# Layer 1's merge gates as seven block products in pairs, and four smaller edits, in a two-layer hybrid attention kernel

## The chip, the cores and the metric

The kernel runs on one core of one Trainium2 chip, as one program. The metric is its device time in microseconds; less is better. Of the core's engines the text speaks of PE (TensorE matmul; PEld is its weight load), DVE (VectorE), ACT (ScalarE), POOL (GpSimd), and SP, whose queue issues the DMA transfers.

## The reference, cut to what matters

Two layers are computed over 512 latent tokens (width 1024); 256 context tokens are also updated in layer 0, and only read in layer 1.

```python
h = rms_norm(x, norm_g) * (1 + scale) + shift
qc, kvc, kr, dq, dk, dv, sq, sk, sv, z, gm = split_cols(h @ w_in)      # one input projection
ya = dense_attend(...)      # mla: qc (384) and kvc (256) are RMS-normed first, then projected up
yb = diff_post(diff_attend(...))
yc = swa_latent(...)
def merge_branches(ys, z, gm, w_branch, w_out):
    for r, y in enumerate(ys):                       # 3 branches, z and gm have 3*1024 columns
        terms.append(sigmoid(gm_r) * ((y * silu(z_r)) @ w_branch[r]))
    return (terms[0] + terms[1] + terms[2]) @ w_out
x = x + gate * merge_branches(...)
return rms_norm(x, final_norm)                       # after layer 1
```

## The kernel before, in words

Everything is float32. For a matmul each operand is split into a rounded part H and a rest L, and a product is three matmuls (`PASS`: H·H, H·L, L·H). ACT writes H, DVE writes L as "source minus H" (`split_to`, and `split` in `weight_stream` for weights). A weight block of 128 output columns is a tile `ws` as loaded, and two tiles `wh` (H and L) after the split; six `wh` tiles go round. The activations h lie in 16 tiles `s` (8 of 128 features, H and L), with the context tokens in columns 0 to 255 and the latents in 256 to 767.

**The order of the work.** A planner (`Plan`) runs while the program is built: generators yield the time from which they can go on, `P.tick` and `P.advance` move its clock by a cost for each matmul (`mm_cost`), and every engine's instructions are emitted in the order in which it takes them. On the chip each engine runs its instructions strictly in that order, and waits on semaphores. PE's order interleaves two streams: the attention units (`stream_a`) and the projections (`stream_b`). Stream b's order is written out by hand: `SEQ[l]` for the first part of layer l (Q, K, V: the windowed branch; c0 to c2, cn, p: mla's queries; l0, l1, ln, u, w: mla's keys and values; k, q, v: the differential branch; z20 and so on: silu gates computed early), then `MID` in layer 0 and `BR` in layer 1 for the merge. Short PE work that hangs on a chain goes through `P.pe` as a piece, which is taken before the streams as soon as it is ready. `HAM` and `advance` model that matmuls cost double after a stretch in which PE did little.

**The merge in layer 0** (`gates_by_pairs`). z (silu gate) and g (merge gate) of two blocks of 128 columns are computed together: the two weight blocks are cut in halves of the features, h in halves of the features and of the tokens, and instead of eight block products seven are made (a Winograd form). `seven` makes four sums of weight halves (S1 to S4) and splits all seven operands, 11 DVE operations on 128x512 for each pair; `sums` makes the sums of h (T1 to T4) once. `pair_entry` issues seven products of 12 matmuls over half the tokens (384 columns each), and its `chain` puts the results together with one ACT copy and seven DVE additions, while PE goes on. The results go to DRAM (`s_d`, `g_d`), and come back when `u_entry` (y·silu(z)) and `b_entry` (times `w_branch`, times the gate) need them.

**The merge in layer 1** (`gates`). Eleven of the 24 z blocks are in `SEQ[1]`. The other 13, and all 24 g blocks, are computed one at a time by `wide`: 24 matmuls of 512 columns each, into one of two wide banks (`wd`).

**The other places that the change touches.** `rms_cols` normalises the latents of mla: it sums squares over partitions with matmuls of two columns against `ones` (each stands as two in the trace), then takes the root and spreads it by transposes. `s_pieces` scores one row of 128 queries at a time; a differential row takes both wide banks, one for each of its two maps. `begin` loads the first rows and the modulation weights. `out_entry` ends with the final norm.

Of the kernel before, what the change touches and what calls it, by code (L numbers as in the profile page):

```python
# [16 lines left out]
F32 = mybir.dt.float32  # L17
# [10 lines left out]
INF = float("inf")  # L28
NS, NT, NWS, NWH = 46, 9, 2, 6
MID = 'z25 z26 z27 z16 t z17 z00 z01 T pg20g21+ pg22g23+ pg24g25+ pg26g27+ pz02z03+ pz04z05+ pz06z07+ pg10g11+ pg12g13+ u20 pg14g15+ u21 pg16g17+ u22 pg00g01+ u23 pg02g03+ u24 pg04g05 u25 pg06g07! u26 u27 b20 b21 u10 u11 b22 u12 u13 b23 u14 b24 u15 b25 u16 b26 u17 b27 u00 u01 b10 u02 u03 b11 u04 u05 b12 u06 b13 u07 b14 b15 b16 b17 b00 b01 b02 b03 b04 b05 b06 b07'  # L30
BR = ['z0 z3 g0 z7 z4 z5 z2 z6 g2 z1 g5 b0 b2 g1 g4 g3 b3 b1 b4 g6 g7 b6 b5 b7', 'z7 z0 z5 z2 g0 g2 z4 z1 z3 g1 z6 g4 b1 g3 b0 b4 g5 g6 b3 b5 b6 g7 b2 b7', 'z4 z0 z7 z1 z2 z6 g0 z3 z5 g2 g1 g3 g6 g4 g5 b1 b3 b2 b4 g7 b0 b5 b6 b7']
# [9 lines left out]
DEPTH = 2  # L41
START = 1
# [3 lines left out]
SEQ = ["cn Q0 K0 V Q1 c0 c2 c1 Q2 Q3 cr p1 z20 p2 p0 p3 Q4 z21 K1 Q5 z22 Q6 z23 k1 Q7 v0 k0 v1 q0 z24 q1 k3 q2 k2 l0 v2 l1 ln lr q3 q5 k4 q4 k5 v3 k6 q6 u0 q7 k7 w0 z11 z10 u1 w1 z12 w2 z13 z14 u2 z15 u3 w3",  # L46
       "K0 V cn Q0 Q1 c1 c0 c2 Q2 cr p0 p1 Q3 p2 p3 z20 Q4 K1 z21 Q5 z22 Q6 z23 Q7 v0 l0 k0 q0 k1 z24 v1 k2 q1 q2 q3 l1 lr k3 q4 v2 ln k4 k5 q5 v3 k6 q6 k7 q7 u0 z10 w0 z11 u1 z12 z13 u2 w2 w1 z15 z14 u3 w3"]
# [81 lines left out]
class Plan:  # L129
# [43 lines left out]
    def pe(self, ready, cost, emit):  # L173

        done = When()
        self.pieces.append((ready, cost, emit, done))
        yield done
        return done.t

    def advance(self, cost):  # L180
# [15 lines left out]
    def run(self, a, b):  # L196
# [8 lines left out]
        while live or self.pieces or self.waiting:  # L205
            self.flush()
            for i, (ready, cost, emit, done) in enumerate(self.pieces):
                if at(ready) <= self.now - TOPE:
                    del self.pieces[i]
                    emit()  # L210
                    self.advance(cost)
# [25 lines left out]
def hybrid_kernel(tc, x_in, c_in, ctx_in, c_ctx, w_mod, b_mod, norm_g, w_in, q_norm, w_uq, kv_norm, w_ukv,  # L237
# [645 lines left out]

    def normalise(t, p, r):
# [23 lines left out]
    def soft_diff(u, row, m, p, rel, t):  # L908
        lo, hi = u["span"]
# [46 lines left out]
    def s_pieces(u):  # L956
        for row in u["rows"]:
            row["t"] = When()
# [5 lines left out]
            maps = 2 if u["kind"] == "diff" else 1  # L964
            yield lambda: max(wd.gate(maps), at(u["ready"]), at(row["ready"]), room(2)())
# [355 lines left out]
    def rms_cols(raw, sq, nt, nfeat, gcol, outH, outL, done, times, tk0=0):  # L1321
# [4 lines left out]
        def emit():  # L1326
            o["p"], o["r"] = bk.take()
            for i in range(ntk):
                for k in range(nt):
                    c = (i + tk0) * 128  # L1330
                    mm(o["p"][:, 2 * i:2 * i + 2], sq[k][:, c:c + 128], ones, k == 0, k == nt - 1)
        t = yield from P.pe(lambda: max([bk.gate()] + [w.t for w in times]), nt * ntk * 215.0, emit)
# [40 lines left out]
    def build_layer(o):  # L1373
# [851 lines left out]
```

## Time and profile before

| | us |
|---|---|
| three runs | 2669.98, 2665.61, 2669.41 (median 2669.41) |
| the profiled execution | 2665.98, span 2664.2 |
| PE busy | 2594.5 (97% of the span), 16419 matmuls |
| DVE busy | 1750.0 (66%) |
| ACT busy | 1386.0 (52%) |
| mean granted TensorE clock | 0.994 |

PE is busy in 97% of the span, so the time is PE's work plus the places at which PE stands still or runs at a lower clock. The span falls into the start (0 to 45 us), layer 0's attention with projections (45 to 1010), its merge (1010 to 1490), the step to layer 1 (1490 to 1540), layer 1's attention with projections (1540 to 2292), its merge (2292 to 2655) and the tail.

### The profile page before, as it was taken

The numbers are of one execution on the slowest core, as the hardware profiler recorded it, in microseconds if no ns is written. First come the engines' busy times: TensorE is split into PE (matmuls) and PEld (weight loads), VectorE is DVE, ScalarE is ACT, GpSimd is POOL, SyncE is SP. The second block draws the span as 40 slices with busy tenths as digits, with TensorE's granted clock in tenths as the row PEclk, the third lists the DMA queues.
The fourth block names the chain that finished last, engine by engine and source line by source line (L and its number), as shares of the span: only waits on it lengthen the run. The fifth ranks groups of instructions, "written<-read, shape, count | busy, mean of one in ns | idle before, by whom it ended". The sixth has DMA issues, their size and how long they took to land. (4 is left out here: it accounts for less than half of the span.)

```text
span 2664.2 us, 42925 instructions
## 1 busy us (share of the span) xinstructions
PE 2594.5 (97%) x16419; PEld 2284.4 (86%) x16419; DVE 1750.0 (66%) x3292; ACT 1386.0 (52%) x2791; POOL 172.1 (6%) x371
## 2 busy tenths in 40 slices
PE   7999999999999999999999999999999999999998
PEld 5988898888889888899888888898888789888887
DVE  4777786757786657677454478887577777534535
ACT  5667775646665543344222267776555656422323
POOL 1110110111110000000000011110110100000000
PEclk9999999999999999999999999999999999999999
DMA  7223211121122545455753423222211233344433
GB/s 243 49 77 108 67 45 52 45 59 29 52 82 73 170 150 154 145 159 162 245 204 111 134 78 103 78 57 61 60 50 44 62 94 105 106 125 126 127 97 132
DMA packets 341009, 274.48 MB, mean 103 GB/s; under 512 B 26134, under 2 KB 297588, under 8 KB 340804
## 3 DMA queue, kind: packets, MB, share of 16 engines
q1 hardware_dynamic: 340160, 271.41, 34.4%
q8 instruction: 129, 2.11, 0.3%
q14 instruction: 76, 0.62, 0.1%
q0 software_dynamic: 416, 0.30, 0.1%
q10 hardware_dynamic: 228, 0.03, 0.0%
HBM read 221.72 MB, written 49.95 MB: 102 GB/s over the span
## 5 line engine op out<-in xcount | busy, mean ns | idle before, releaser
L530 PE MATMUL bk<-s,wh 128*128 128x512 f32 (+2 forms) x5262 | 1052.4, 350 | 19.5 <-DVE pt L324 14.4
L530 PEld LDWEIGHTS bk<-s,wh 128*128 128x128 f32 x5262 | 852.3, 189 | 122.6 <-DVE pt L324 21.8
L324 DVE TENSOR_TENSOR wh<-ws,wh 128x1024 fp32r<-128x1024 f32 (+4 forms) x305 | 312.9, 1031 | 352.2 <-ACT wh L310 350.6
L530 PE MATMUL wd<-s,wh 128*128 128x512 f32 (+1 forms) x2616 | 537.2, 367 | 2.9 <-ACT s L310 2.7
L530 PEld LDWEIGHTS wd<-s,wh 128*128 128x128 f32 x2616 | 452.2, 189 | 84.2 <-ACT s L310 3.3
L310 ACT ACTIVATE wh<-ws 128x1024 fp32r<-128x1024 f32 (+4 forms) x305 | 273.0, 900 | 390.4 <-PE wd L530 252.7
L310 ACT ACTIVATE pt<-bk 128x512 fp32r<-128x512 f32 (+4 forms) x619 | 348.5, 580 | 170.6 <-PE bk L1000 113.4
L324 DVE TENSOR_TENSOR pt<-bk,pt 128x512 fp32r<-128x512 f32 (+4 forms) x469 | 295.7, 645 | 83.4 <-ACT pt L310 66.4
L530 PE MATMUL bk<-wh,s 128*128 128x256 f32 (+1 forms) x2304 | 331.3, 295 | 1.0 <-DVE pt L324 0.4
L530 PEld LDWEIGHTS bk<-wh,s 128*128 128x128 f32 x2304 | 300.1, 191 | 11.7 <-DVE pt L324 1.1
L530 PE MATMUL bk<-pt,s 128*128 128x256 f32 x1888 | 279.3, 287 | 8.4 <-DVE pt L324 6.4
L530 PEld LDWEIGHTS bk<-pt,s 128*128 128x128 f32 x1888 | 252.9, 191 | 31.3 <-DVE pt L324 14.7
L530 PE MATMUL wd<-s,s 128*128 128x256 f32 (+5 forms) x1872 | 270.5, 329 | 1.8 <-ACT s L310 1.6
L310 ACT ACTIVATE s<-wd,ti 128x768 f32<-128x768 f32 (+1 forms) x240 | 195.3, 817 | 126.6 <-DVE ti L912 73.8
L530 PEld LDWEIGHTS wd<-s,s 64*128 64x128 f32 (+2 forms) x1872 | 210.8, 188 | 29.2 <-issue 6.2
L1000 PE MATMUL bk<-ident,s 128*128 128x128 f32 x1472 | 209.1, 274 | 4.9 <-DVE s L324 1.7
L310 ACT ACTIVATE s<-s,ti 128x513 f32<-128x513 f32 (+6 forms) x256 | 184.0, 726 | 27.1 <-DVE ti L948 13.2
L1000 PEld LDWEIGHTS bk<-ident,s 128*128 128x128 f32 x1472 | 170.7, 142 | 26.0 <-DVE s L331 3.3
L310 ACT ACTIVATE s<-s 128x768 fp32r<-128x768 f32 (+2 forms) x98 | 75.2, 768 | 198.3 <-DVE s L324 178.4
L310 ACT ACTIVATE yo<-bk 128x256 f32<-128x256 f32 (+1 forms) x200 | 72.4, 383 | 158.6 <-PE bk L530 157.6
L310 ACT ACTIVATE s<-bk 128x256 fp32r<-128x256 f32 (+6 forms) x305 | 119.7, 426 | 61.1 <-PE bk L530 59.7
L948 DVE CUSTOM_DVE_ANT_0 s<-wd,s,sinkt 128x512 f32<-128x512 f32 (+2 forms) x160 | 116.2, 745 | 48.4 <-PE wd L530 48.1
(115 smaller groups left out, 1828.6 us busy)
## 6 DMA issues: line engine op xcount, KB each, us to landing
ws<-in_w_in_dram SPq DMA_DIRECT2D x167, 512.0 KB
ws<-in_w_branch_dram SPq DMA_DIRECT2D x48, 512.0 KB
s<-s SPq DMA_DIRECT2D x48, 384.0 KB
s<-in_w_mod_dram SPq DMA_DIRECT2D x48, 256.0 KB
s<-in_w_mod_dram SPq DMA_DIRECT2D x32, 384.0 KB
y<-yo SPq DMA_DIRECT2D x80, 128.0 KB
g<-s SPq DMA_DIRECT2D x24, 384.0 KB
s<-y SPq DMA_DIRECT2D x24, 384.0 KB
```

Source lines behind the costliest of these rows:

```text
L310: lambda: nc.scalar.activation(out=out, in_=in_, func=func, scale=scale, **kw))
L324: t = yield from dve(ready, lambda: nc.vector.tensor_tensor(out=out, in0=a, in1=b, op=op), n)
L530: nc.tensor.matmul(o, lhsT=l, rhs=r, start=first, stop=last)
L948: t = yield from dve(t, lambda: nc.vector.tensor_tensor_reduce(out=pt_[:, 0:n], in0=p[:, lo:hi], in1=mk, scale=1.0, scalar=sk, op0=ALU.add ...
L1000: nc.tensor.transpose(out=pp[:, j * 256 + ri2 * 128:j * 256 + ri2 * 128 + 128], in_=row["P"][:, c:c + 128], identity=ident)
```

## The change

1. **Layer 1's gates as pairs.** `gates` and `BR` are gone; the code of `gates_by_pairs` now serves both layers, with halves of 256 tokens in layer 1. `MID[1]` sets the order: the 13 remaining z first, each by the ordinary `z_pre` (512 columns, result to DRAM), with the sums T1 to T4 (`t`) and six u among them, then 12 pairs of g, then u and b. T2 and T3 of layer 1 are written over the context columns of h.
2. **First loads.** `keep_busy` gives PE eight groups of four transposes of the identity, planned from 29 us on, 1.1 us apart. They use a bank and wait for nothing else.
3. **Context rows.** The eight differential units over context queries score both rows of queries at once (`score_two`): both rows of a map lie in one wide bank.
4. **Latent norms.** In `rms_cols` the sums over partitions are issued in groups of two token blocks, as pieces of their own, and the planner counts a tenth of their time as PE activity.
5. **Order.** Both `SEQ` lists are other orders of the same steps. In the final norm the multiplication by `final_norm` stands behind the sum for the root instead of ahead of it.

```diff
-MID = 'z25 z26 z27 z16 t z17 ...'
-BR = ['z0 z3 g0 z7 z4 z5 z2 ...']
+MID = ['z25 z26 z27 z16 t z17 ...', 'z25 z26 z27 t z16 z17 z00 u20 z01 u21 z02 u22 z03 u23 z04 u24 z05 u25 z06 z07 pg20g21+ pg22g23+ pg24g25+ pg26g27+ pg10g11+ pg12g13+ pg14g15+ pg16g17+ pg00g01+ pg02g03+ pg04g05+ u26 u27 pg06g07+! u10 u11 b20 u12 b21 u13 b22 ...']
...
+WARM = (29000.0, 1100.0, 8)
...
-SEQ = ["cn Q0 K0 V Q1 c0 c2 c1 Q2 Q3 cr p1 z20 ...", "K0 V cn Q0 Q1 c1 c0 c2 Q2 cr p0 ..."]
+SEQ = ['Q0 K0 V Q1 c2 c0 c1 Q2 cn Q3 p1 z20 cr ...', 'K0 V Q0 Q1 c0 c1 c2 Q2 cn cr p1 ...']
...
-            self.ham[i] = self.ham.get(i, 0.0) + d / f
+            self.ham[i] = self.ham.get(i, 0.0) + d / f * share
...
+    def score_two(rows):
+        o = [wd.take() for _ in range(2)]
+        ps_ = [[row["passes"](m) for m in range(2)] for row in rows]
+        for j in range(2):
+            for i in range(len(ps_[0][0])):
+                for m in range(2):
+                    q, k = ps_[j][m][i]
+                    mm(o[m][0][:, 512 * j:512 * j + 256], q, k[:, 0:256], i == 0, i == len(ps_[0][0]) - 1)
...
-        def emit():
-            o["p"], o["r"] = bk.take()
-            for i in range(ntk):
...
-        t = yield from P.pe(lambda: max([bk.gate()] + [w.t for w in times]), nt * ntk * 215.0, emit)
+        for i0 in range(0, ntk, 2):
+            def emit():
+                if i0 == 0:
+                    o["p"], o["r"] = bk.take()
+                for i in range(i0, min(i0 + 2, ntk)):
...
+            t = yield from P.pe(lambda: max([bk.gate() if i0 == 0 else 0.0] + [w.t for w in times]), nt * min(2, ntk - i0) * 112.0, emit, 0.1)
...
+                    else:
+                        XB["T2"][s][k], XB["T3"][s][k] = hs[i][k][:, 0:hw], hs[i][k + 4][:, 0:hw]
...
-        (gates_by_pairs if cx else gates)()
...
-                        if l == 1:
+                        if l == 1 and not final:
                             t = yield from tt(t, x, x, o.fn[h][0][:, cc:cc + n], ALU.mult)
...
                             t, r = yield from rstd(t2, s4[tk][:, 0:c + 1])
+                            t = max(t, (yield from tt(t2, x, x, o.fn[h][0][:, cc:cc + n], ALU.mult)))
...
+    def keep_busy():
+        for i in range(WARM[2]):
+            def emit():
+                p, r = bk.take()
+                for c in range(4):
+                    nc.tensor.transpose(out=p[:, c * 128:c * 128 + 128], in_=ident, identity=ident)
+                r.t = P.now
+            yield from P.pe(lambda: max(WARM[0] + i * WARM[1], bk.gate()), 448.0, emit)
```

How the change moves instructions, at the places that the prediction speaks of.

**PE, at the end of layer 1's attention.** Names: `bk` and `wd` are banks, `pt` and `s` data, `wh` split weights. Before, the last product of attention (128x256, into `bk`) is followed by the wide blocks, 1401 matmuls of 512 columns:

```order
L530 MATMUL bk_68<-pt_25160,s_24478 128x256
L530 MATMUL bk_68<-pt_25155,s_24479 128x256
L530 MATMUL wd_71<-s_16278,wh_24632 128x512
L530 MATMUL wd_71<-s_16279,wh_24632 128x512
L530 MATMUL wd_71<-s_16278,wh_24633 128x512
L530 MATMUL wd_71<-s_16280,wh_24632 128x512
```

Now, behind attention, 249 of these (z) stand into `bk`, then the pairs, 1008 matmuls of 256 columns in one stretch, then 576 of 512 columns (b). The step from z to the pairs:

```order
L529 MATMUL bk_66<-s_16314,wh_25567 128x512
L529 MATMUL bk_66<-s_16315,wh_25567 128x512
L529 MATMUL bk_66<-s_16314,wh_25568 128x512
L529 MATMUL bk_69<-s_16300,wh_25617 128x256
L529 MATMUL bk_69<-s_16301,wh_25617 128x256
L529 MATMUL bk_69<-s_16300,wh_25618 128x256
```

Over the whole program the 24 g blocks (576 matmuls of 512 columns) are replaced by the 1008 of 256, and the 13 z move from `wd` to `bk`.

**DVE, in the same part.** Before, for each block of 512 columns one split of a weight (`wh`, 128x1024) and one to three operations on a result:

```order
L324 TENSOR_TENSOR wh_26639<-ws_26567,wh_26638 128x1024
L324 TENSOR_TENSOR wh_26674<-ws_26603,wh_26673 128x1024
L331 SCALAR_TENSOR_TENSOR s_26633<-s_26633,wd_71 128x512
L324 TENSOR_TENSOR s_26633<-s_26633,s_26631 128x512
L331 SCALAR_TENSOR_TENSOR s_26634<-s_26633,s_26631 128x512
L324 TENSOR_TENSOR wh_26710<-ws_26642,wh_26709 128x1024
```

Now 18 operations for each pair: 11 on weights of the next pair (128x512) and seven that read a bank and add (128x256). From one pair:

```order
L323 TENSOR_TENSOR s_26133<-ws_26131,s_26133 128x512
L323 TENSOR_TENSOR pt_26233<-bk_67,pt_26231 128x256
L323 TENSOR_TENSOR wh_26314<-ws_26131,wh_26313 128x512
L323 TENSOR_TENSOR ws_26131<-pt_26281,ws_26131 128x512
L323 TENSOR_TENSOR pt_26232<-bk_66,pt_26231 128x256
L323 TENSOR_TENSOR pt_26282<-ws_26131 128x512
L323 TENSOR_TENSOR s_26229<-bk_67,pt_26232 128x256
```

The third addition of a pair (`pt_26232<-bk_66`, after the fourth product) now stands behind the split of the next pair's A11 and the sum S2; it frees the bank that the seventh product takes.

**PE, the norm of mla's queries in layer 0.** The rows `<-ones` are the sums over partitions. Before, 18 of them stand in one stretch; its last three and what follows:

```order
L530 MATMUL bk_67<-ones,s_1070 128x2
L530 MATMUL bk_67<-ones,s_1400 128x2
L530 MATMUL bk_67<-ones,s_1072 128x2
L530 MATMUL bk_66<-pt_1577,s_687 128x256
L530 MATMUL bk_66<-pt_1582,s_687 128x256
```

Now they stand in three groups of six, with four attention products of 256 columns between two groups; from the end of the first group:

```order
L529 MATMUL bk_68<-ones,s_1104 128x2
L529 MATMUL bk_68<-ones,s_1430 128x2
L529 MATMUL bk_68<-ones,s_1102 128x2
L529 MATMUL bk_69<-pt_1607,s_719 128x256
L529 MATMUL bk_69<-pt_1612,s_719 128x256
```

In layer 1 the norm of the keys' latents stays one stretch of 12 such rows, as before; in layer 0 it is now three groups of four.

**PE, the first loads.** Before, the last modulation weights (`sil`), the columns (`selt`) and the first projection:

```order
L666 MATMUL bk_69<-s_305,sil 32x512
L666 MATMUL bk_69<-s_307,sil 32x512
L678 MATMUL bk_67<-selt,pt_435 128x2 x4
L530 MATMUL bk_68<-s_160,wh_437 128x512
L530 MATMUL bk_68<-s_161,wh_437 128x512
```

Now, with the transposes (`<-ident`) in between; three more groups of four stand ahead of this piece, and two behind it:

```order
L665 MATMUL bk_69<-s_305,sil 32x512
L2135 MATMUL bk_68<-ident 128x128 x4
L665 MATMUL bk_69<-s_307,sil 32x512
L2135 MATMUL bk_66<-ident 128x128 x4
L677 MATMUL bk_67<-selt,pt_454 128x2 x4
L2135 MATMUL bk_68<-ident 128x128 x4
L529 MATMUL bk_66<-s_160,wh_446 128x512
```

More of the change, by code (lines that the diff above doesn't have):

```diff
@@ L171, in on, with pe, advance @@
         return t + 135.0
[L173 removed]
+    def pe(self, ready, cost, emit, share=1.0):
         done = When()
[L176 removed]
+        self.pieces.append((ready, cost, emit, done, share))
         yield done
         return done.t
[L180 removed]
+    def advance(self, cost, share=1.0):
         while cost > 0.0:
@@ L206, in run @@
             self.flush()
-            for i, (ready, cost, emit, done) in enumerate(self.pieces):
+            for i, (ready, cost, emit, done, share) in enumerate(self.pieces):
                 if at(ready) <= self.now - TOPE:
@@ L210, in run @@
                     emit()
-                    self.advance(cost)
+                    self.advance(cost, share)
                     done.t = self.now + 200.0
@@ L908, in soft_diff @@
     def soft_diff(u, row, m, p, rel, t):
-        lo, hi = u["span"]
+        lo, hi = row.get("span", u["span"])
         n = hi - lo
@@ L957, in s_pieces @@
         for row in u["rows"]:
+            if "span" in row:
+                continue
             row["t"] = When()
@@ L964, in s_pieces, with both @@
             maps = 2 if u["kind"] == "diff" else 1
+            if u["kind"] == "diff" and len(u["kts"]) == 2:
+                if row is not u["rows"][0]:
+                    continue
+                u["rows"][1].update(t=When(), Pm=[None, None], tm=[When(), When()], i=1)
+                yield lambda: max(wd.gate(2), at(u["ready"]), room(4)())
+                for j, r_ in enumerate(u["rows"]):
+                    r_["span"] = (512 * j, 512 * j + 256)
+                for m, (p, rel, t) in enumerate(score_two(u["rows"])):
+                    half = [When(), When()]
+                    def both(half=half, rel=rel):
+                        yield lambda: max(w.t for w in half)
+                        rel.t = max(w.t for w in half)
+                    for r_, h_ in zip(u["rows"], half):
+                        P.spawn(soft_diff(u, r_, m, p, h_, t), RANK[1])
+                    P.spawn(both(), 0)
+                continue
             yield lambda: max(wd.gate(maps), at(u["ready"]), at(row["ready"]), room(2)())
@@ L1793, in all_ @@
[L1793 to L1805 removed]
+                    else:
+                        XB["T2"][s][k], XB["T3"][s][k] = hs[i][k][:, 0:hw], hs[i][k + 4][:, 0:hw]
+                        XB["T4"][s][k] = own[i][k // 3][:, k % 3 * hw:k % 3 * hw + hw]
+                        XB["T1"][s][k] = own[i][2 - k // 3][:, (2 - k % 3) * hw:(3 - k % 3) * hw]
@@ new lines, in all_, with sums_last, chain @@
+            def all_():
+                for k in range(4):
+                    yield from whole(k)
+            P.spawn(all_())
+            return
+            yield
+        def sums_last():
+            def chain():
+                for k in range(4):
+                    yield lambda: 0.0 if t1s[k] is not None else INF
+                    x, rr, t = t1s[k]
+                    rr.t = XB["T1"]["t"][k].t = yield from split_to(max(t, P.now), x, XB["T1"]["H"][k], XB["T1"]["L"][k], psum=False)
+            P.spawn(chain())
+            return
+            yield
@@ new lines, in build_layer @@
+        for k in MID[l].split():
+            if k == "t":
+                entry(sums, need=12 if cx else 6, keep=2)
+            elif k == "T":
+                entry(sums_last)
+            elif k[0] == "p":
+                pair_entry(*[(k[i], int(k[i + 1]), int(k[i + 2])) for i in (1, 4)], last="!" in k, apart="+" in k)
+            elif k[0] == "z":
+                z_pre(int(k[1]), int(k[2]))
+            else:
+                {"u": u_entry, "b": b_entry}[k[0]](int(k[1]), int(k[2]))
+            if l == 0 and k[0] in "pbz":
+                some_mod(1)
```

381 lines of the change are left out of this document (136 added, 245 removed).

## The prediction

> **What bounds the kernel now.** I read the page's shares first, then the waits of PE, then the busy times by part of the program. Columns of the last: length, busy time (and instructions) of PE, PEld, DVE, ACT, POOL, then the granted clock, the DMA share and GB/s.
>
> ```profile
> span 2664.2 us, 42925 instructions
> PE 2594.5 (97%) x16419; PEld 2284.4 (86%) x16419; DVE 1750.0 (66%) x3292; ACT 1386.0 (52%) x2791; POOL 172.1 (6%) x371
> ```
> ```profile
> PE bk L530 <- DVE pt L324: 21.2, 33, 2.7
> ```
> ```profile
> 45.00:830.00 785.00, 769.84 (x5376) 690.43 (x5376) 576.05 (x1254) 501.64 (x1115) 85.87 (x198) 0.99 0.23 63
> 1010.00:1260.00 250.00, 242.12 (x1436) 228.86 (x1435) 182.20 (x319) 102.76 (x177) 0.00 (x0) 1.00 0.50 151
> 1540.00:2292.00 752.00, 738.45 (x4934) 652.36 (x4935) 563.18 (x1077) 488.84 (x989) 71.41 (x142) 1.00 0.26 72
> 2292.00:2655.00 363.00, 362.69 (x1692) 304.20 (x1690) 160.29 (x202) 110.17 (x152) 1.12 (x2) 1.00 0.42 121
> ```
>
> PE is busy in 97% of the span: time goes down if PE has less to do, stands still less, or runs less at half clock. In the part that the change rewrites, 2292 to 2655 us, PE stands still for 363.00 − 362.69 = 0.3 us, so PE work taken out there is time, as long as the other engines keep up: DVE is 160.29/363 = 44% busy there. Elsewhere PE stands still for 15.2 us in layer 0's attention up to 830 us, 7.9 us in layer 0's pairs and 13.6 us in layer 1's attention; most of what releases it is a DVE result (`pt`).
>
> **The pairs: PE's side.** The pitch of matmuls comes from two long unbroken stretches (count, then first and last start): 512 columns in layer 1's merge, 256 columns in the first value projection.
>
> ```profile
> L530 PE MATMUL wd<-s,wh x1326: 389/389/389, 2299.7 to 2600.0; 128*128 128x512 f32 x190
> L530 PE MATMUL bk<-wh,s x121: 283/283/283, 60.7 to 75.1; 128*128 128x256 f32 x121
> ```
>
> 300.3/1325 = 0.227 us for 512 columns, 14.4/120 = 0.120 us for 256. So 24 g blocks cost 576 × 0.227 = 130.8 us and the 12 pairs 1008 × 0.120 = 121.0 us: −9.8 us. The product count falls by an eighth, but a 256-column matmul costs more than half of a 512-column one, which takes back almost half of that (130.8/8 = 16.4 us). The 13 z keep their matmuls, so 0.
>
> [...]
>
> **The pairs: DVE's side.** Layer 0 runs the same 18 DVE operations for a pair, with 384 columns. One pair's period there, and two rows that give the step from 384 to 256 columns:
>
> ```profile
> 1150.95:1165.51 14.56, 14.56 (x86) 14.56 (x85) 10.56 (x19) 6.13 (x10) 0.00 (x0) 1.00 0.46 136
> ```
> ```profile
> L324 DVE TENSOR_TENSOR pt<-bk,pt 128x384 f32<-128x384 f32 x45 | 24.7, 552 | 4.7 <-PE bk L530 4.7
> L324 DVE TENSOR_TENSOR pt<-bk,pt 128x256 f32<-128x256 f32 x16 | 6.7, 419 | 1.8 <-PE bk L530 1.8
> ```
>
> DVE works 10.56 of 14.56 us (the x19 counts one at the edge), PE never stops. In layer 1 the seven additions shrink by 133 ns: 10.56 − 0.93 = 9.63 us, against 84 × 0.120 = 10.08 us of PE. DVE goes from 44% to 96%; 0.45 us a pair is left for everything that it waits for. The tightest loop: the fourth product's end frees `wh` for the next A11, ACT copies, DVE splits and makes S2, and only then the third addition frees the bank of the seventh product. Layer 0's rows for it:
>
> ```profile
> 1164.84 0.63 ACT L310 ACTIVATE wh<-ws 128x512 fp32r<-128x512 f32 x1 [3.52 <-PE bk L530]
> 1165.51 0.69 DVE L324 TENSOR_TENSOR wh<-ws,wh 128x512 fp32r<-128x512 f32 x1 [2.06 <-ACT wh L310]
> 1166.23 0.69 DVE L324 TENSOR_TENSOR ws<-pt,ws 128x512 f32<-128x512 f32 x1
> 1166.96 0.69 DVE L324 TENSOR_TENSOR pt<-ws 128x512 f32<-128x512 f32 x1
> ```
>
> From ACT's start to the third addition's start 2.12 us (1166.96 − 1164.84), its own 0.42, so 2.54 us; with the fifth and sixth product between (2 × 12 × 0.120 = 2.88 us), some 0.3 us remain for the semaphores at both ends. Bounds: 0, if it just fits, and 12 × (9.63 + 4.00 − 10.08) = +42.6 us, if DVE's 4.00 us of waiting per pair in layer 0 stayed. A middle mark is the 7.9 us that PE stood still over layer 0's 15 pairs (0.5 each, 6 us for 12). The nearest row has PE busy in 14.56 of 14.56, so I stay near zero: 0.12 a pair, **+1.5 us**.
>
> **What follows the pairs.** b now loads g and u from DRAM in layer 1 as it does in layer 0, where PE once waited for such a load:
>
> ```profile
> 1270.56 0.96 DVE L324 TENSOR_TENSOR s<-s,s 128x768 f32<-128x768 f32 x1 [5.16 <-DMA s<-s]
> 1272.44 0.79 PE L530 MATMUL wd<-s,wh 128*128 128x512 f32 x1 [2.55 <-ACT s L310]
> ```
>
> Bounds 0 and 2.55 us + 1.7 for the half clock that followed. The new order has the last u of the first branch ahead of the last pair, a pair earlier than layer 0: **+1.0 us**. SP's queue carries 86 more issues, spread over 360 us; the DMA share there was 0.42, so I put them at nothing; uncovered, they are this same wait.
>
> **The clock.** The clock is seen by stretches of 3.41 us. Three pairs of a stretch and the next, one that follows the norm of the keys in layer 1, and three around that norm in layer 0:
>
> ```profile
> 36.80:40.21 3.41, 1.78 (x10) 1.27 (x10) 0.93 (x2) 1.40 (x3) 0.00 (x0) 1.00 0.96 320
> 40.21:43.62 3.41, 2.90 (x7) 2.32 (x8) 1.84 (x4) 3.41 (x8) 0.00 (x0) 0.50 0.80 247
> 139.20:142.61 3.41, 3.41 (x30) 3.28 (x28) 1.01 (x2) 0.73 (x3) 0.00 (x0) 1.00 0.48 143
> 142.61:149.44 6.83, 6.83 (x34) 6.83 (x34) 0.99 (x4) 0.38 (x1) 2.06 (x6) 0.50 0.00 0
> 1538.66:1542.08 3.42, 2.47 (x22) 2.27 (x21) 3.37 (x8) 3.24 (x5) 0.55 (x1) 1.00 0.42 101
> 1542.08:1545.49 3.41, 3.25 (x23) 2.72 (x21) 3.41 (x7) 3.36 (x7) 0.00 (x0) 1.00 0.90 283
> 1996.05:1999.46 3.41, 3.41 (x10) 2.53 (x9) 0.39 (x1) 0.00 (x0) 1.32 (x1) 0.50 0.91 251
> 559.04:569.28 10.24, 10.17 (x66) 9.02 (x65) 2.40 (x3) 2.29 (x4) 1.32 (x1) 1.00 0.25 66
> ```
> ```profile
> 140.05 5.33 PE L530 MATMUL bk<-ones,s 128*128 128x2 f32 x36
> 561.04 2.96 PE L530 MATMUL bk<-ones,s 128*128 128x2 f32 x24
> 1992.91 2.74 PE L530 MATMUL bk<-ones,s 128*128 128x2 f32 x24
> ```
>
> A stretch of two-column matmuls counts as idle: PE was "busy" all through 139.20 to 142.61, and the clock was halved behind it. Two stretches at half clock cost 6.83/2 = 3.4 us; one costs 1.7.
> - Norm of the queries, layer 0: three groups of 12 (36 in the trace) with 0.48 us of real products between. Both halvings would go at this phase; a stretch that begins with the first group would hold too little again. Bounds −3.4 and 0: **−2.5 us**, nearer to both going.
> - Norm of the keys, layer 1: still 24 in one run. Whether it lowers the clock hangs on where the stretch begins; the same 24 in layer 0, at 561.04, had full clock around them. Bounds −1.7 and +1.7: **−0.7 us**.
>
> **The first loads.** PE's rows there:
>
> ```profile
> 35.27 1.05 PE L666 MATMUL bk<-s,sil 128*32 128x512 f32 x2 [0.68 <-DMA s<-in_w_mod_dram]
> 37.00 1.05 PE L678 MATMUL bk<-selt,pt 128*128 128x2 f32 x8 [0.69 <-ACT pt L310]
> 39.46 0.73 PE L530 MATMUL bk<-s,wh 128*128 128x512 f32 x2 [1.40 <-ACT wh L310]
> 40.72 3.90 PE L530 MATMUL bk<-s,wh 128*128 128x512 f32 x10 [0.53 <-DVE wh L324]
> ```
>
> A transpose takes 0.11 us (in the stretch from 1538.66, 15 of them fill 1.67 us, row below), a group of four 0.44: 3.5 us for eight, and the gaps shown are 3.3 us together. If the groups count as activity, the half clock from 40.21 goes, up to −1.7 us; the first ten projections then wait for DVE's splits sooner, and one or two groups may stand where PE had work (+0.9 at most). **−0.8 us.** Without the gaps as cover it would be +3.5.
>
> ```profile
> 1538.66:1542.08 3.42, 1.67 (x15) 1.67 (x16) 0.00 (x0) 1.00 0.42 101
> ```
>
> The row is the transposes' share of that stretch: without them PE had 2.47 − 1.67 = 0.8 us of work in it, as little as the two stretches that half clock followed had beside their two-column matmuls (142.61 − 140.05 = 2.56, and 3.41 − 2.56 = 0.85; 1.78 − 1.05 = 0.73), and the clock stayed at 1.00. So transposes count here. [...]
>
> **The tail.** The multiplication by the final norm stands ahead of the sum for the root:
>
> ```profile
> 2658.38 0.42 DVE L324 TENSOR_TENSOR s<-s,pt 128x256 f32<-128x256 f32 x1 [0.64 <-ACT pt L310]
> 2658.72 0.15 DVE L742 TENSOR_REDUCE ti<-ti 128x1 f32<-128x3 f32 x1
> 2658.91 0.15 DVE L743 TENSOR_SCALAR ti<-ti 128x1 f32<-128x1 f32 x1
> 2659.20 0.55 POOL L744 TENSOR_TENSOR ti<-ti,mhalf 128x1 f32<-128x1 f32 x1 [2.77 <-DVE ti L743]
> ```
>
> Behind it, its 0.42 us fit beside POOL's 0.55: 2658.72 − 2658.38 = **−0.3 us**.
>
> **Order and context rows.** The two `SEQ` orders and `score_two` keep every operation; they redraw where PE stands still. Two drawings of the same kind of program stood still for 15.2 of 785 us and 13.6 of 752 us, 1.9% and 1.8%, so another drawing gives about the same: 0, with ±5 us (a third of either).
>
> **The sum.** −9.8 + 1.5 + 1.0 − 2.5 − 0.7 − 0.8 − 0.3 = −11.6 us. The profiled execution took 2665.98 us (span 2664.2 and 1.8 around it), 3.4 below the median of the runs and 0.4 above the fastest, so the sum gives 2654.4 for an execution like it and 2657.8 against the median. I take the middle, **2656 us**.
>
> **Rivals.**
> - *DVE is the bound of the pairs in part.* For: 96% load, and 0.3 us in the loop. Against: layer 0's pairs never stopped PE in the rows shown. At 0.5 to 1.2 us a pair, 6 to 14 us in place of 1.5: 2661 to 2669.
> - *Slower: ACT and DVE wait for each other in every pair.* All 18 operations are fixed in order, so if layer 0's 4.00 us of DVE waiting a pair stayed in part, each pair would lengthen for PE too. The price is 12 × the excess; the pairs gain nothing from 10.9 us a pair on (130.8/12), and the kernel is slower by over 0.2% from about 11.8 us a pair; the full 13.63 gives 2656 + 41 = 2697. Against: in layer 0 DVE waits because it is ahead of PE, and that slack may shrink without harm.
> - *The clock edits do not do what they say.* The halvings at 142 and 1996 stay and the transposes do not count: +4 us, 2660.
> - *The new order stands still for less.* If the stalls of layer 0's pairs and both attention parts (36.7 us) fall by a quarter: −9, 2647. For: these are waits for single results. Against: 1.9% and 1.8% above.
>
> **How the numbers follow.** Forecast (2650 to 2662) 0.52; DVE the bound in part 0.16; clock edits fail 0.10; less standing still 0.10; slower through the pairs 0.09; a worse drawing, +8 to +13 us, 0.03. A difference under 0.2% (5.3 us) can hardly be told from none, as the runs spread by 4.4 us. Faster: 0.52 + 0.10 + 0.10 + a quarter of 0.16 = 0.76; same: 0.12 + 0.03 = 0.15; slower 0.09. The range from 2647 to 2668 leaves out the slow case, half of the lower one and a little more, 0.16.
>
> **What would show it.** Products: 1008 matmuls of 256 columns in 121 to 124 us without a break; PE waiting for DVE `pt` or `wh` there by more than 3 us would refute the DVE step. Clock: no 0.50 in the 10 us behind the two-column groups of layer 0, nor at the first projection. Tail: TENSOR_REDUCE straight behind the last square. The prediction is wrong if PE's idle time outside the pairs grows by more than 8 us.

## The result, and the profile after

The changed kernel takes 2654.27 us (median of four runs, 2651.18 to 2656.58) against 2669.69: a ratio of 0.9945, with a 95% interval from 0.9931 to 0.9959. The prediction was 2656. The execution with the profile is the slowest of the four, 2656.58 us, so between the two profiles only 9.5 us of the 15.4 are seen.

The page after: PE has 464 matmuls more and 7.5 us less to do, DVE 95 us more.

```profile
span 2654.7 us, 44487 instructions
PE 2587.0 (97%) x16883; PEld 2301.9 (87%) x16883; DVE 1844.8 (69%) x3530; ACT 1418.6 (53%) x2881; POOL 173.1 (7%) x371
```

The parts of the changed kernel (columns as in the prediction): the attention parts of layers 0 and 1, the 13 z, the pairs, b with the output projection, and last one period of 84 matmuls from the middle of the pairs.

```profile
45.00:830.00 785.00, 770.66 (x5402) 691.47 (x5401) 576.42 (x1253) 503.05 (x1119) 86.13 (x197) 0.99 0.22 62
1545.00:2292.00 747.00, 733.86 (x4919) 649.66 (x4919) 554.88 (x1066) 484.74 (x983) 70.94 (x141) 1.00 0.25 70
2292.00:2347.70 55.70, 55.70 (x248) 46.10 (x247) 44.81 (x84) 24.55 (x45) 0.00 (x0) 1.00 0.66 196
2347.70:2468.60 120.90, 120.90 (x1008) 120.78 (x1007) 108.08 (x211) 65.08 (x119) 0.00 (x0) 1.00 0.55 157
2468.60:2645.90 177.30, 175.73 (x866) 149.12 (x865) 107.74 (x153) 55.26 (x80) 1.27 (x2) 1.00 0.61 197
2398.12:2408.21 10.09, 10.09 (x87) 10.09 (x86) 9.17 (x19) 5.40 (x10) 0.00 (x0) 1.00 0.55 156
```

The fourth row is the change: 1008 matmuls in 120.9 us and PE never still, with DVE busy for 108.08/120.90 = 89%. The first and the last pair hold fewer DVE operations, so the period from the middle is the fairer figure: 9.17 of 10.09 us, 91%. PE stands still once behind the pairs, for a multiplication of b; the row ahead of it is its neighbour on PE:

```profile
2468.76 16.54 PE L529 MATMUL wd<-s,wh 128*128 128x512 f32 x72
2486.88 1.39 PE L529 MATMUL wd<-s,wh 128*128 128x512 f32 x5 [1.57 <-ACT s L309]
```

To see where the time came from, I cut each trace at the starts of the same matmuls: the first value projection (V0), the long unbroken stretch of layer 0's pairs, layer 1's value projection (V1), the first z behind layer 1's attention, the output projection, and the last matmul. The table holds the executions with a profile; those whose names are explained below are listed here once.

| us | start to V0 | V0 to pairs | pairs to V1 | V1 to z | z to output | output | tail | span | runs: median (spread) |
|---|---|---|---|---|---|---|---|---|---|
| before | 60.7 | 1058.2 | 439.5 | 733.7 | 317.6 | 44.7 | 9.8 | 2664.2 | 2669.7 |
| changed | 60.9 | 1058.7 | 440.5 | 731.0 | 310.0 | 44.7 | 8.8 | 2654.7 | 2654.3 (2651.2 to 2656.6) |
| pairs alone | 59.5 | 1059.1 | 442.6 | 733.2 | 308.8 | 44.7 | 9.8 | 2657.6 | 2659.6 (2658.5 to 2661.5) |
| no groups | 60.8 | 1058.8 | 441.9 | 735.3 | 308.7 | 44.7 | 8.8 | 2659.1 | 2660.6 (2658.5 to 2662.3) |
| sums whole | 60.3 | 1056.2 | 441.2 | 726.7 | 308.9 | 44.7 | 8.8 | 2646.8 | 2649.0 (2648.5 to 2650.9) |
| old orders | 60.7 | 1065.8 | 443.8 | 736.0 | 309.1 | 44.7 | 8.8 | 2668.8 | 2674.2 (2668.9 to 2677.9) |
| old tail | 60.5 | 1055.5 | 442.0 | 733.2 | 308.7 | 44.7 | 9.8 | 2654.4 | 2654.6 (2652.7 to 2659.2) |
| whole, rows apart | 60.9 | 1055.3 | 442.4 | 727.2 | 309.4 | 44.7 | 8.8 | 2648.7 | 2651.6 (2649.4 to 2657.8) |
| DVE + 2 | 60.8 | 1056.5 | 439.9 | 734.5 | 309.3 | 44.7 | 8.8 | 2654.5 | 2656.6 (one) |
| DVE + 4 | 59.9 | 1057.9 | 438.0 | 733.1 | 315.1 | 44.7 | 9.1 | 2657.7 | 2659.5 (one) |
| 64 columns | 60.9 | 1051.6 | 440.9 | 728.2 | 309.2 | 44.7 | 8.8 | 2644.3 | 2648.6 (2645.6 to 2649.4) |
| whole, no groups | 60.2 | 1058.5 | 442.4 | 728.1 | 308.9 | 44.7 | 8.8 | 2651.7 | 2652.1 (2648.8 to 2653.5) |
| whole, new cost | 60.6 | 1054.1 | 439.7 | 729.6 | 308.9 | 44.7 | 8.8 | 2646.4 | 2650.2 (2648.5 to 2657.7) |
| 64 columns, rows apart | 61.6 | 1054.2 | 440.0 | 728.2 | 309.6 | 44.7 | 8.8 | 2647.1 | 2647.9 (2645.5 to 2649.0) |

Between the two profiles the merge gave 7.5 us, layer 1's attention 2.7 and the tail 1.0; layer 0 took 1.8 back. The experiments were taken in four other sessions than the changed kernel, each with its own runs of before, to which its ratio is taken (medians 2669.3 to 2670.9, single runs from 2661.6 to 2676.7). Beside that spread a difference of 2 us in one profile, or between medians of two sessions, says little; a column that keeps apart in every row says more.

### The profile page after: what moved, and what is told of

Its sections match the earlier page's. It is cut to its first block, busy times and chain, and to the rows that moved or that the text cites. A ratio compares the mean times of both kernels' runs of the same rounds, so it can differ in the third digit from the quotient of the medians.

```text
span 2654.7 us, 44487 instructions
## 1 busy us (share of the span) xinstructions
PE 2587.0 (97%) x16883; PEld 2301.9 (87%) x16883; DVE 1844.8 (69%) x3530; ACT 1418.6 (53%) x2881; POOL 173.1 (7%) x371
## 5 line engine op out<-in xcount | busy, mean ns | idle before, releaser
L529 PE MATMUL bk<-s,wh 128*128 128x512 f32 (+2 forms) x6582 | 1248.6, 342 | 12.7 <-DVE pt L323 9.0
L529 PEld LDWEIGHTS bk<-s,wh 128*128 128x128 f32 x6582 | 1031.4, 190 | 126.9 <-DVE pt L323 16.2
L323 DVE TENSOR_TENSOR wh<-ws,wh 128x1024 fp32r<-128x1024 f32 (+4 forms) x317 | 307.1, 974 | 238.8 <-ACT wh L309 237.4
L309 ACT ACTIVATE pt<-bk 128x512 fp32r<-128x512 f32 (+5 forms) x631 | 352.9, 576 | 172.6 <-PE bk L1031 115.4
L323 DVE TENSOR_TENSOR pt<-bk,pt 128x512 fp32r<-128x512 f32 (+4 forms) x505 | 310.4, 628 | 87.4 <-ACT pt L309 70.8
L529 PE MATMUL wd<-s,wh 128*128 128x512 f32 (+1 forms) x1728 | 335.2, 356 | 4.9 <-ACT s L309 4.2
L529 PEld LDWEIGHTS wd<-s,wh 128*128 128x128 f32 x1728 | 287.3, 191 | 52.5 <-ACT s L309 5.6
L309 ACT ACTIVATE s<-s 128x768 fp32r<-128x768 f32 (+3 forms) x122 | 90.2, 740 | 223.6 <-DVE s L323 220.1
L309 ACT ACTIVATE s<-bk 128x256 fp32r<-128x256 f32 (+6 forms) x318 | 128.2, 433 | 55.2 <-PE bk L529 54.0
```

The costliest lines, as they stand in the source:

```text
L309: lambda: nc.scalar.activation(out=out, in_=in_, func=func, scale=scale, **kw))
L323: t = yield from dve(ready, lambda: nc.vector.tensor_tensor(out=out, in0=a, in1=b, op=op), n)
L529: nc.tensor.matmul(o, lhsT=l, rhs=r, start=first, stop=last)
```

## The experiments

**The pairs alone.** The changed kernel with all else taken back:

```diff
-SEQ = [the new orders]
+SEQ = [the old orders]
-        P.spawn(keep_busy())
-            if u["kind"] == "diff" and len(u["kts"]) == 2:
+            if False:
...   (rms_cols and the final norm as in the kernel before)
```

> The kernel before with layer 1's gates as pairs and nothing else of the change (both orders of the steps, the norms of the latents, the first loads, the context rows and the tail as before). Theory: the pairs save what their matmuls save, wherever they stand: from the first z behind attention to the last b, 317.4 us becomes 309 to 310 (pairs -9.5, stalls behind them +1 to +2), and the time falls by 7.5 us (5 to 10). Rival A, the pairs gain nothing alone and the change's gain is the new order and the clock: the time falls by less than 3 us and PE waits for DVE between 256-column matmuls. Rival B, the other edits cost something and hide part of the pairs: the time falls by 12 us or more.

2659.64 us, ratio 0.9962 (0.9948 to 0.9975): 10 us less than before, the upper end of what was expected, and neither rival. Z to output took 308.8 us instead of 317.6. The profile behind z (busy time and mean, then the idle time ahead):

```profile
L530 PE MATMUL wd<-s,wh 128*128 128x512 f32 x576 | 131.0, 389 | 0.5 <-ACT s L310 0.5
L530 PE MATMUL bk<-s,wh 128*128 128x256 f32 x1008 | 121.1, 283 | 0.0
```

So the pairs are worth 8.0 to 8.9 us in every kernel of the table that has them without the stall of 1.57 us shown above or more work for DVE, and alone they bring two thirds of what the whole change gained. The 1.57 us are no fixed price: the other profiles have 0.3 to 1.4 us there, and the two with more work for DVE none.

**No groups of transposes at the first loads.**

```diff
-        P.spawn(keep_busy())
```

> The changed kernel without the eight groups of transposes at the first loads. Theory, transposes count as activity and the groups' work takes back what the clock gains: a stretch of 3.4 us at half clock comes back between 37 and 44 us, and the first value projection starts at 60.9 +/- 0.5 us with them or without; the time changes by less than 1 us. Rival, the prediction's term: it starts 0.8 us later without them or more. Rival, the groups don't count as activity: no half clock comes back, and the projection starts 1 to 2 us sooner without them.

The half clock came back. This kernel at its first projection, then the changed kernel:

```profile
37.33:40.75 3.42, 1.96 (x12) 1.44 (x12) 1.50 (x4) 2.75 (x4) 0.00 (x0) 1.00 0.99 345
40.75:44.16 3.41, 3.41 (x9) 2.63 (x9) 1.93 (x3) 3.41 (x12) 0.00 (x0) 0.50 0.94 273
```
```profile
38.57:41.98 3.41, 3.31 (x23) 2.53 (x22) 2.42 (x3) 2.94 (x9) 0.00 (x0) 1.00 0.91 314
41.98:45.40 3.42, 3.42 (x20) 2.62 (x19) 3.19 (x12) 3.42 (x13) 0.56 (x1) 1.00 0.87 267
```

All four profiles without the groups have 0.50 there, none of the ten with them. Yet V0 starts at 60.8 us without them and at 60.9 with them: with the groups in front of it the first projection begins about 2 us later (at 40.99 against 39.04 us). That much was expected. What wasn't: the runs take 2660.56 us, 6.3 more, although behind the first projections PE's order is the same row for row. Between these two profiles the loss lies in layer 1's attention (4.3 us) and behind layer 0's pairs (1.4), but that doesn't place it: layer 1's attention has one stretch at half clock in the profile of the changed kernel and four in this one, and three later profiles with the groups and the same PE order have three or four too.

**The sums of the norms in one stretch.**

```diff
-        for i0 in range(0, ntk, 2):
-            ... two token blocks a piece, 112 ns each, a tenth of it as activity
+        def emit():
+            ... all token blocks in one piece, 215 ns each
```

> The changed kernel with the sums of the latent norms in one stretch each, costed as before. Theory, cutting the stretch moves the halvings instead of removing them: the two stretches at half clock at 622 us (norm of the keys in layer 0) go, and behind the norm of the queries (144 us) there are two instead of one; the time changes by -1.7 us (between -4 and +2). Rival, the prediction's terms: the cut is worth 2.5 us at the queries and 0.7 at the keys of layer 1, so the time is 3 us longer.

2648.99 us, ratio 0.9926 (0.9911 to 0.9941), 5.3 under the changed kernel: the sign of the theory, and three times its size. The halvings at the norms are the smaller part of it. V1 to z is 726.7 us, and the table parts here: 731.0 to 735.3 in the five profiles with the new orders and the cut, 726.7 to 729.6 in the six without the cut. PE stands still for 12.6 to 13.1 us of that part with the cut and for 9.4 to 10.4 without, and the clock is halved for one to four stretches against one or two. All five with the cut have this stall, of 2.9 to 3.3 us, with half clock behind it (PE first, then DVE):

```profile
1634.31 0.60 PE L1031 MATMUL bk<-ident,s 128*128 128x128 f32 x4
1638.19 0.66 PE L1031 MATMUL bk<-ident,s 128*128 128x128 f32 x4 [3.27 <-DVE pt L323]
```
```profile
1634.40 1.41 DVE L323 TENSOR_TENSOR s<-pt,s 64x512 fp32r<-64x512 f32 x2
1635.84 1.69 DVE L323 TENSOR_TENSOR wh<-ws,wh 128x1024 fp32r<-128x1024 f32 x2
1637.45 0.68 DVE L323 TENSOR_TENSOR pt<-bk,pt 128x512 fp32r<-128x512 f32 x1
```

PE has nothing but a transpose that waits for `pt`, and `pt` stands on DVE behind two results and two weight splits, 3.05 us of work. Without the cut PE waits there for 1.0 to 1.4 us, and 25 us later for 2.7 in place of 1.3. Taken together, this part of the program gives 0.6 to 1.5 of the some 3 us; the rest lies further on. At the norms themselves, the cut changed this:

```profile
140.97:144.38 3.41, 3.41 (x32) 3.41 (x32) 0.00 (x0) 0.00 (x0) 0.00 (x0) 1.00 0.10 17
144.38:147.80 3.42, 3.42 (x18) 3.42 (x18) 1.69 (x5) 0.38 (x1) 2.06 (x6) 0.50 0.00 0
618.84:622.25 3.41, 3.29 (x30) 3.01 (x30) 2.26 (x4) 2.01 (x5) 0.00 (x0) 1.00 0.39 89
622.25:629.08 6.83, 6.83 (x24) 5.31 (x21) 3.47 (x7) 1.87 (x4) 1.32 (x1) 0.50 0.11 32
```

Behind the queries one halved stretch in place of two; behind layer 0's keys two where the kernel before had none. Over all profiles with the new orders, those with 64 columns aside: at the queries 1, 2, 1, 2, 2 with the cut and 0, 2, 2, 1 without; at layer 0's keys 2 in each of the five with the cut, and 1, 0, 1, 1 without. So the cut changes little at the queries (1.6 stretches on average against 1.25) and costs more than one at layer 0's keys (2 against 0.75).

**Only the cut undone, the new cost kept.**

```diff
-        for i0 in range(0, ntk, 2):
+        for i0 in range(0, ntk, ntk):
```

> The changed kernel with the sums of the norms in one stretch, but with the planner's new cost for them (112 ns each and a tenth of it as activity), so that only the cut is undone. With the old cost too it took 2649.0 us, and layer 1's attention 726.7 us against 731.0 to 735.3 in the changed kernel, which has a stall of 3.3 us at 1635 us. Theory, the cut makes the loss (the norm ends later, and the transposes behind it wait for DVE): 2648 to 2651 and no stall over 2 us there. Rival, the new cost makes it: the stall stays and the time is 2653 to 2657.

2650.19 us (2648.49 to 2657.67). By the time alone this run doesn't decide, since one of its four executions is slower than the slowest of the changed kernel. The trace does: V1 to z is 729.6 us, PE stands still for 10.4 us of it, and for 1.4 us at the place of the stall, as in the other profiles without the cut. So the cut makes that loss, and not its cost in the plan. Why the cut leads to this order on DVE is open.

**The old orders in the changed kernel.**

```diff
-SEQ = [the new orders]
+SEQ = [the old orders]
```

> The changed kernel with the two old orders of the steps of stream b. Prediction's term: 0 +/- 5 us; PE stands still for as long in both attention parts. Theory from the two traces: from the first value projection to the first pair of layer 0 the new order gained 1.5 us although its clock was lower for longer, and in layer 1 up to the first z some 1 us beside the clock; with the old orders the time is 2 to 5 us longer. Rival, the drawing matters more than that in the one or the other direction: over 5 us.

2674.21 us, ratio 1.0016 (1.0005 to 1.0028): 20 us longer than the changed kernel and no faster than before, the rival's case. V0 to pairs took 1065.8 us and V1 to z 736.0. In the first PE stands still for 32.7 us against 24.0 in the changed kernel. The largest wait of PE over the whole span (total, times, longest), then that of the changed kernel:

```profile
PE bk L530 <- DVE pt L324: 25.0, 36, 2.2
```
```profile
PE bk L529 <- DVE pt L323: 15.0, 29, 1.8
```

The same old orders without the other edits took 2659.6 us (the pairs alone). So beside the old orders those edits (groups, context rows, cut, tail) together cost 14.6 us, and most of the 20 us is not what the new orders gain by themselves: an order and the edits that shift the plan's times go together. Which of the edits costs beside the old orders is open.

**The old tail.**

```diff
-                        if l == 1 and not final:
+                        if l == 1:
-                            t = max(t, (yield from tt(t2, x, x, o.fn[h][0][:, cc:cc + n], ALU.mult)))
```

> The changed kernel with the multiplication by the final norm ahead of the sum for the root, as before; PE's and ACT's order are those of the changed kernel row for row. From the last matmul to the end of the span the changed kernel took 8.8 us and the kernel before 9.8. Theory: the move of the multiplication is all of it, so 9.8 us come back. Rival, the prediction's term: 0.3 us, so 9.1. This run also shows the changed kernel's other parts a second time: if the places of the half clock are fixed by the program, the two stretches at 622 us, the two at 875 and the one at 144 are there again; if they hang on where the stretches of 3.41 us happen to begin, some differ and the first matmul of the first value projection, relative to the stretches, does too.

The tail is 9.8 us again: the move is worth 1.0 us, not 0.3. The runs took 2654.56 us (2652.68 to 2659.20), 0.3 more than the changed kernel; their spread hides 1 us. This kernel's last two token blocks, from POOL's power to the scaling on DVE, then those of the changed kernel:

```profile
2645.95 0.55 POOL L743 TENSOR_TENSOR ti<-ti,mhalf 128x1 f32<-128x1 f32 x1 [2.65 <-DVE ti L742]
2646.53 0.49 DVE L2070 TENSOR_SCALAR s<-s,ti 128x512 f32<-128x512 f32 x1 [0.66 <-POOL ti L743]
2649.27 0.55 POOL L743 TENSOR_TENSOR ti<-ti,mhalf 128x1 f32<-128x1 f32 x1 [2.77 <-DVE ti L742]
2649.85 0.49 DVE L2070 TENSOR_SCALAR s<-s,ti 128x512 f32<-128x512 f32 x1 [0.73 <-POOL ti L743]
```
```profile
2646.46 0.66 POOL L743 TENSOR_TENSOR ti<-ti,mhalf 128x1 f32<-128x1 f32 x1 [2.31 <-DVE ti L742]
2647.15 0.49 DVE L2071 TENSOR_SCALAR s<-s,ti 128x512 f32<-128x512 f32 x1 [0.44 <-POOL ti L743]
2649.55 0.60 POOL L743 TENSOR_TENSOR ti<-ti,mhalf 128x1 f32<-128x1 f32 x1 [2.44 <-DVE ti L742]
2650.18 0.49 DVE L2071 TENSOR_SCALAR s<-s,ti 128x512 f32<-128x512 f32 x1 [0.44 <-POOL ti L743]
```

From scaling to scaling it takes 3.32 us with the old order and 3.03 with the new. The blocks follow one another on DVE, whose adds for the next stand behind the scaling of this one, so the saving counts for each: over the four blocks of the tail the first scaling comes 0.3 us sooner against the last matmul, and the last scaling 9.04 us behind the first in place of 9.78.

The run is also a second execution of the changed kernel's PE order, and with the next two there are four. Their halvings differ: at 144 us 1, 1, 2, 2 stretches; at 1977 us 0, 1, 2, 1. One stall makes it plain. In both executions PE stands still for 3.1 to 3.2 us at 221. The rows are cut at the clock's own stretches, those of the changed kernel counted on from the halved one that begins at 144.38; the changed kernel first, then the old tail:

```profile
219.47:222.89 3.42, 1.54 (x7) 0.94 (x5) 0.81 (x1) 1.85 (x4) 0.22 (x2) 1.00 0.81 231
222.89:226.30 3.41, 2.17 (x14) 1.96 (x15) 2.65 (x8) 3.28 (x7) 0.00 (x0) 1.00 0.99 328
226.30:229.71 3.41, 3.41 (x25) 3.25 (x24) 1.87 (x5) 0.64 (x2) 0.00 (x0) 1.00 0.98 312
```
```profile
220.16:223.58 3.42, 0.43 (x2) 0.01 (x1) 1.72 (x2) 2.83 (x5) 0.00 (x0) 1.00 0.76 211
223.58:226.99 3.41, 3.16 (x12) 2.87 (x13) 2.33 (x7) 2.29 (x6) 0.00 (x0) 0.50 0.98 306
```

Here the clock falls where one of its stretches holds nearly all of the stall (PE busy for 0.43 of 3.42 us), and stays where two share it (1.54 of 3.42 and 2.17 of 3.41). Within an execution the halved stretches begin a whole number of steps apart (in the changed kernel 772 steps of 3.413 us from 14.68 to 2649.77 us), and this grid lies differently against the program in each of the four, whose first halved stretch began at 14.7, 15.4, 17.4 and 16.3 us of the span.

**More work for DVE in each pair.** The last addition of a pair is done three times, or five times:

```diff
+                    for _ in range(2 if l == 1 else 0):     # or 4
+                        t12 = yield from tt(t12, c12, bank[6], x4, ALU.add)
```

> The changed kernel with the last addition of each of layer 1's pairs done three times instead of once: 2 more DVE operations of 128x256, some 0.75 us a pair; PE's order is the same. DVE worked 108.1 us in the 120.9 us of the pairs, 9.0 a pair, and comes to some 9.75 of 10.08. Theory: DVE's waiting gives way and PE's stretch of 1008 matmuls stays at 121 to 122 us. Rival, the prediction's middle mark (each pair loses 0.5 us where DVE is 96% busy): 127 us or more.

> The same with the last addition done five times: 4 more, some 1.5 us a pair, DVE 10.5 us a pair against PE's 10.08. Theory: DVE is the bound now and PE waits for the difference, 12 x 0.4 = 5 us: the stretch takes 125 to 128 us. Rival, DVE's waiting of 4.00 us a pair seen in layer 0 can't be squeezed out: 12 x (10.5 + 1 - 10.08) or more, over 137 us. Rival, the splits for the next pair are far enough ahead to take it up over 12 pairs: under 123 us.

These are single runs. The stretch of the pairs with two more, a period from its middle, and PE's waits in the stretch; then the same with four more:

```profile
2348.20:2470.30 122.10, 121.16 (x1008) 120.86 (x1007) 118.30 (x235) 67.39 (x119) 0.00 (x0) 1.00 0.55 158
2399.09:2409.28 10.19, 10.19 (x88) 10.19 (x87) 10.09 (x21) 5.74 (x11) 0.00 (x0) 1.00 0.55 156
```
```profile
PE bk L529 <- DVE pt L323: 0.9, 1, 0.9
```
```profile
2345.40:2472.70 127.30, 123.56 (x1008) 122.15 (x1007) 123.13 (x258) 65.69 (x120) 0.00 (x0) 0.99 0.54 156
2398.48:2409.12 10.64, 10.64 (x89) 10.51 (x88) 10.64 (x24) 5.56 (x11) 0.00 (x0) 1.00 0.56 162
```
```profile
PE bk L529 <- DVE wh L323: 3.7, 4, 2.9
```

With two more DVE is busy for 97% of the stretch and 99% of a period in its middle, and the pairs lose 1.2 us, 0.9 of it in one wait ahead of the last product. With four more they take 127.3 us, the 125 to 128 of the theory: in the middle DVE never rests (10.64 of 10.64 us). Not all of the loss is waiting, though: PE waits for 3.7 us, 2.9 of them ahead of the last ten matmuls, and these then run at half clock, which adds some 1.1 us (2.3 us in place of 1.2). So DVE's own work is the bound, and its waits of layer 0 give way.

**Context rows apart again**, beside the sums in one stretch (the `if False:` of the first experiment):

> The changed kernel with the sums of the latent norms in one stretch (2649.0 us as run before, 5.3 under the changed kernel) and, beyond that, the context rows of the differential branch scored one at a time as in the kernel before. Theory: the stall of 2.6 to 3.2 us at 870 us in layer 0 (PE wd, s,s), seen in all three runs with both rows in one bank and the new order, belongs to the new scoring, with the half clock that follows: the time falls by 2 to 6 us, to 2643 to 2647. Rival, the stall belongs to the new order of the steps (its weights landed late) and stays: the time is 2648 to 2652. Rival, the redrawn order stands still elsewhere: over 2652.

2651.56 us (2649.44 to 2657.79): nothing gained, the first rival's time. Yet the stall at 870 us, 1.9 to 3.2 us in the profiles with the new order and the rows together, is gone here, so it does belong to the new scoring. It takes the new order as well, since the run with the old orders scores both rows together and has no such stall. From V0 to V1 the time is 1497.7 us against 1497.4 all the same.

**64 columns instead of two.**

```diff
-                    mm(o["p"][:, 2 * i:2 * i + 2], sq[k][:, c:c + 128], ones, k == 0, k == nt - 1)
+                    mm(o["p"][:, 64 * i:64 * i + 64], sq[k][:, c:c + 128], wones, k == 0, k == nt - 1)
```

> The changed kernel with the sums of the latent norms in one stretch (2649.0 us as run before), and these sums against 64 columns of ones instead of two (all columns but the first are not used); every engine's order is the same. The two-column matmuls stand 0.114 us apart (24 in 2.74 us). Theory, what counts as activity is columns streamed, and the pitch is set by loading the weights, as it is for the transposes of 128 columns at 0.11: the pitch stays at 0.11 to 0.12, the stretches at half clock behind the norms (seen at 142, 622 and 1975 us in one execution or another, three to five stretches of 3.41 us in each) go, those behind plain stalls stay, and the time falls by 3 to 7 us, to 2642 to 2646. Rival, the pitch grows with the columns: 108 matmuls at 0.16 or more, 5 us longer, and the gain is eaten: 2648 to 2652. Rival, a float32 matmul of few columns counts as idle whatever its width: 2649 +/- 1.5.

The norm of the queries with two columns (sums whole), then with 64:

```profile
138.91 4.07 PE L529 MATMUL bk<-ones,s 128*128 128x2 f32 x36
```
```profile
139.56 4.12 PE L530 MATMUL bk<-wones,s 128*128 128x64 f32 x36
```

The wider matmuls cost the same. The clock around them, with two columns (whole, rows apart) and with 64:

```profile
138.61:142.02 3.41, 3.41 (x30) 3.19 (x28) 1.07 (x2) 0.86 (x3) 0.00 (x0) 1.00 0.73 115
142.02:145.43 3.41, 3.41 (x17) 3.41 (x18) 0.17 (x1) 0.00 (x0) 0.04 (x1) 0.50 0.02 5
```
```profile
139.15:142.57 3.42, 3.42 (x31) 3.33 (x29) 0.50 (x2) 0.30 (x1) 0.00 (x0) 1.00 0.61 95
142.57:145.98 3.41, 3.41 (x32) 3.41 (x31) 0.69 (x2) 0.38 (x1) 2.01 (x6) 1.00 0.02 5
```

Every halving behind a latent norm is gone, in both kernels that have this edit; the four profiles with two columns and the sums in one stretch have two to four such stretches each. The time did less than expected: 2648.55 us against 2648.99, within the spread, though the profiled execution is 2.5 us shorter. Where the rest went is open.

**The sums in one stretch, no groups**, the second and the third experiment's edits together.

> The changed kernel with the sums of the norms in one stretch, without the eight groups of transposes. From the changed kernel they could be taken away at a cost of 6.3 us (2660.6 against 2654.3), although the first value projection started at the same time (60.8 and 60.9 us) and PE's order behind it is the same; no row shows where 6 us come from, except for the clock (0.990 and 0.991 against 0.991 to 0.994). Theory, the 6.3 us are where the stretches of 3.41 us happened to begin, and the groups are worth nothing by themselves: the time is within 2 us of 2649.0. Rival, the groups set where these stretches begin, and the effect is general: 2653 or more. Half clock at the first projection: comes back in either case.

2652.09 us (2648.78 to 2653.53), 3.1 longer than with the groups, between the theory and the rival, and measured in another session than the run it is compared with. By the medians the groups are worth 6.3 and 3.1 us in the two pairs of kernels, and not at the place where they stand. One reading: the half clock ties the program to the clock's stretches. Without the groups, V0 comes 17.1, 17.1, 16.7 and 17.7 us after the end of the halved stretch, and all four have two halved stretches at the queries' norm, while with the groups there are none to two. This fits, but no run takes it by itself, and it stays open.

**The best two together**, 64 columns and rows apart.

> The two best ideas so far together, to see whether they add: the sums of the norms in one stretch against 64 columns of ones, and the context rows scored one at a time. With two columns this order took 2651.6 us (spread 2649.4 to 2657.8; its profiled execution 2650.5, with three stretches at half clock behind the norms, 142 and 1975 us, and no stall at 870). Theory: the three stretches go (5.1 us) in every execution, and the spread shrinks: 2645 to 2648, and no execution over 2652. Rival: what the halvings leave goes to waits for DVE, as the medians of the version with both rows together suggest (2649.0 and 2648.6 with two and with 64 columns): 2650 to 2652.

2647.93 us (2645.50 to 2648.98), ratio 0.9912 (0.9895 to 0.9928): as expected, the fastest here by median, 6.3 us under the changed kernel, though not apart from 64 columns alone.

## Why the prediction was right

The time came out as forecast, in part by luck: terms of the wrong size, some of the wrong sign, cancelled.

- *Pairs, PE's side, −9.8:* right. The 1008 matmuls take 121.1 us where the 576, of the 1401 that took 317.6 us before, took 130.6: −9.5.
- *Pairs, DVE's side, +1.5:* 0. The step that failed is DVE's work of a pair: 9.17 us, 91%, not 9.63 and 96%. The operation at the edge of the quoted window is not the reason, for it begins where the window ends and adds nothing to the 10.56. The rest of layer 0's time, which the prediction kept, was too much. The rows show one reason. An operation of 128x512 takes 0.68 to 0.69 us. In the quoted window three that depend on the one of 128x512 before them start 0.72 us behind it (at 1151.67, 1152.40 and 1160.71), in the period of layer 1 one does (at 2405.61); what else stands behind one of 128x512 without a wait starts 0.60 to 0.65 behind it, and so overlaps with it. One behind a wait overlaps with none: DVE waits three times in the quoted window (1.43, 0.37 and 2.06 us) and once in the period of layer 1 (0.89). How the 0.46 us divide wasn't measured. Even at a load of 99% the term would have been +1.2. The slow rival falls: DVE's 4.00 us of waiting a pair were slack.
- *First loads of b, +1.0:* 1.57 here, 0.3 to 1.4 in the others: right.
- *Norm of the queries, −2.5, and layer 1's keys, −0.7:* failed; behind the two-column groups of layer 0 the clock does read 0.50 (144.38 to 147.80 us, 622.25 to 629.08). "A stretch that begins with the first group would hold too little again" was the likelier case, not the bound: at the queries the counts with and without the cut hardly differ. Layer 0's keys, which the prediction took as harmless since they had full clock, got two halved stretches. And in the cut's redrawn order PE stands still for some 3 us more in layer 1. Together the cut costs 4 to 5 us by the medians instead of saving 3.2. The rival "the clock edits fail" named half of this.
- *First loads, −0.8:* the halving goes (1.00 at the first projection in place of 0.50), the groups' own work takes it back, 0 at V0 (60.9 us, 60.8 without them). The 3 to 6 us that the kernel loses without them were not in the sum.
- *Tail, −0.3:* −1.0. The saving was right for a block, and was counted once where four blocks follow one another.
- *Order and context rows, 0 ± 5:* the step that failed most. The changed kernel itself stands still for about as long as before (67.7 us of the span against 69.7), as the term said. But two drawings of one program agreeing in their idle share (1.9% and 1.8%) do not bound a third: with the old orders the changed kernel is 20 us slower, and V0 to pairs runs from 1051.6 to 1065.8 us over the table.

In sums of medians, with the tail from the traces: the pairs −10.0, the tail −1.0, the cut +5.3, the groups −3.1 to −6.3, which leaves −3 to −7 of the −15.4 for orders and context rows. That is a remainder and not a measurement, and the parts don't add strictly, as the old orders show.

## What to carry to other kernels

Price a cut in PE work by its pitch where PE never stops, and the helper engine by its own busy time per period; its waiting is not a price until its work fills the period, which here cost 1.2 us at 99%. An edit that shifts the times of a static planner redraws the rest of the program, and here that was worth as much as the edits (14.6 us beside the old orders): try each with the orders found for it. A saving in a chain that repeats counts once for each link that waits for the one before (1.0 us over the four blocks of the tail, 0.3 for one).

## What was not expected of the hardware

- Widening the sums' matmuls from two to 64 columns of float32 cost next to nothing (4.07 us for 36, 4.12 with 64 columns) and removed the half clock behind them in both profiles that have it.
- One order of PE's work, executed again, meets the half clock in other places: of four executions, three halved it behind the same stall of 3.1 to 3.2 us at 221 us and one did not.
- Eight groups of transposes kept the clock at 1.00 at the first projection in ten of ten profiles, where four of four without them fell to 0.50.
